# Decay column as the bias of an exponential on ScalarE instead of a sum on GpSimd, in a hybrid decoder layer

## The chip, the cores and the metric

The kernel runs on one core of a Trainium2 chip. The metric is the device time of one execution in microseconds; the median of several executions is compared. The core's engines work side by side, each through its own queue in order: TensorE (PE; its weight loads are listed as PEld), VectorE (DVE), ScalarE (ACT) and GpSimd (POOL). SyncE (SP) issues the DMA transfers.

## What is computed

The layer (sequence 512, model width 2048, one sequence) has two parallel branches: sliding-window attention with 32 query heads, and a gated delta rule ("DeltaNet") with 16 key heads and 32 value heads of 128. The change concerns the decay of the second branch:

```python
g = jnp.cumsum(g, axis=-1)
tril = jnp.tril(jnp.ones((C, C), dtype=bool))
decay = jnp.exp(jnp.where(tril, g[..., :, None] - g[..., None, :], -jnp.inf))
...
L = jnp.where(strict, jnp.einsum('bhncd,bhnsd->bhncs', k_beta, k) * decay, 0.0)
...
qk = jnp.where(tril, jnp.einsum('bhncd,bhnsd->bhncs', q, k) * decay, 0.0)
q_dec = q * jnp.exp(g)[..., None]
```

So for each value head a matrix of decays is needed twice: for L, which is inverted, and for qk. The query times the exponential of g is needed once.

## The kernel before

All matrix products are float32, split into a high and a low part: `mm3` (L236) issues three matmuls, L240 to L242, for each pair of tiles. A projection tile of 128 channels by 512 positions (`channel_tile`) is 48 such matmuls that accumulate in one PSUM tile, mm. Its weights come by DMA in tiles raw and are split by `split`: ScalarE casts a half of 128x1024 to whi (L61), VectorE subtracts to get wlo (L62).

The projections follow each other on TensorE without a break, and everything else is woven between them. Each piece of side work is a generator that yields a number; `pump` is called after every second k-step of a projection and resumes each generator that has counted down. The written program gives the priorities, and a scheduler then puts each engine's instructions into the order of its queue, by its own estimate of time. At run time each engine keeps that order and waits by semaphores.

The stages are: startup; the keys of the delta rule (`delta_keys`, with `keys` once for each of 16 groups g of one key head and two value heads e); attention; the heads of the delta rule (`delta_heads`, `queries` and `values` for each of the 16 groups); and two output stages. A solver (`solve`) works on VectorE from the end of the key stage into the first groups of heads; its steps are the lines L737 and L745 on tiles A and atmp.

A decay matrix is made in tile E, 128 partitions by 4 blocks of 128 columns. In `queries` the variable for it is M, and the profile calls it E as well:

- `decay_load` (L695) sends, for head h, the row of g to all partitions by DMA, g_rows to E.
- `decay_mask` (L701) works on GpSimd. L705 adds the column neg_g, which holds minus g for each partition and block: neg_g[:, c, h] for block c. L706 is an affine selection that puts -1e30 into the upper or lower part that is not wanted.
- The exponential is one ScalarE instruction of 128x512 for each E, at L670 in `keys` and L833 in `queries`.
- The result is multiplied on VectorE with the product of keys (L678) or of query and key (L845).

In `queries` GpSimd also multiplies the query with the exponential of g, in tile qe (L839, called qd in the code), after a DMA has brought that row (eg_rows). The value tiles go through a convolution on ScalarE and VectorE: L570, L573 three times, the tanh L578, and L580. TensorE then transposes yv (L281, tile ptv) and ScalarE copies the result (L789). L270 is the eviction of a gate projection (tanh into mth). L660 scales the keys k by a column, L668 copies their transpose kT, and L675 multiplies keys with keys (pkk).

`behind` (L244) adds a dependence for the scheduler alone: the given instruction is not placed ahead of the last matmul that has been written. It adds no wait at run time.

Of the kernel before, what the change touches and what calls it, by code (L numbers as in the profile page):

```python
# [10 lines left out]
AF = mybir.ActivationFunctionType  # L11
ALU = mybir.AluOpType
# [4 lines left out]
P = 128  # L17
# [3 lines left out]
NTB = T // P  # L21
# [24 lines left out]
class Layer:  # L46
# [194 lines left out]
        nc.tensor.matmul(ps, lhsT=wh, rhs=xl, start=False, stop=False)  # L241
        self.last_mm = nc.tensor.matmul(ps, lhsT=wl, rhs=xh, start=False, stop=last)  # L242

    def behind(self, ins):  # L244

        self.tc.add_manual_dep(
            ins.ins, self.last_mm.ins.name, mybir.DependencyInfo(mybir.DependencyClass.NoSync, mybir.DependencyReason.DATA),
            reason="pace",
        )

# [393 lines left out]
    def keys(self, wk, g, ps):  # L644

        nc = self.nc
        y = wk.tile([P, T], F32, tag="y", name="y", bufs=3)
        yield from self.conv(wk, ps, 16 + g, y)
        yield 2
        pt = self.ptp.tile([P, T], F32, tag="tp", name="ptk")  # L650
        self.transpose4(pt, lambda c: y[:, c * P : (c + 1) * P])
        ss = self.sumsq(wk, pt)
        yield 3
        E = [self.decay_load(wk, 2 * g + e) for e in range(2)]
        nc.vector.tensor_scalar(out=ss, in0=ss, scalar1=EPS, scalar2=None, op0=ALU.add)
        rk = self.rsqrt(wk, ss, NTB, "rk")
        yield 4
        k = wk.tile([P, NTB, P], F32, tag="k", name="k")
        for c in range(NTB):
            nc.scalar.activation(k[:, c, :], pt[:, c * P : (c + 1) * P], AF.Copy, scale=rk[:, c : c + 1])  # L660
        for e in range(2):
            self.decay_mask(E[e], 2 * g + e)
        yield 4
        pt = self.ptp.tile([P, T], F32, tag="tp", name="ptkT")
        self.transpose4(pt, lambda c: k[:, c, :])
        nc.sync.dma_start(out=self.k_d[g], in_=k.rearrange("p c d -> p (c d)"))
        kT = wk.tile([P, T], F32, tag="kT", name="kT")
        nc.scalar.copy(out=kT, in_=pt)  # L668
        for e in range(2):
            nc.scalar.activation(E[e], E[e], AF.Exp)  # L670
        yield 2
        pk = self.ptp.tile([P, NTB, P], F32, tag="tp", name="pkk")
        for c in range(NTB):
            sl = slice(c * P, (c + 1) * P)
            nc.tensor.matmul(pk[:, c, :], lhsT=kT[:, sl], rhs=kT[:, sl], start=True, stop=True)  # L675
        nc.sync.dma_start(out=self.kT_d[g], in_=kT)
        for e in range(2):
            nc.vector.tensor_tensor(out=E[e], in0=pk, in1=E[e], op=ALU.mult)  # L678
        yield 2
        for e in range(2):  # L680
            h = 2 * g + e
            b, hl = h // 16, h % 16
            for k2 in range(2):
                s = slice(k2 * HD, (k2 + 1) * HD)
                nc.sync.dma_start(out=self.lt_d[b, k2, hl].rearrange("c j i -> j c i"), in_=E[e][s, :, s])
            nc.sync.dma_start(out=self.lab_d[h], in_=E[e][0:HD, :, HD:P])
        self.keys_done.append(g)
# [10 lines left out]
        self.nc.sync.dma_start(out=E.rearrange("p c i -> p (c i)"), in_=self.g_rows[h].partition_broadcast(P))  # L698
        return E

    def decay_mask(self, E, h):  # L701

        nc = self.nc
        ng = self.neg_g[:, :, h].unsqueeze(2).to_broadcast([P, NTB, P])
        nc.gpsimd.tensor_tensor(out=E, in0=E, in1=ng, op=ALU.add)  # L705
        nc.gpsimd.affine_select(  # L706
            out=E, in_=E, pattern=[[0, NTB], [1, P]], compare_op=ALU.is_ge, fill=NEG, base=0, channel_multiplier=-1
        )

    def solve(self, wk, b, eng):  # L710

# [80 lines left out]
    def queries(self, wk, g, ps, st):  # L792

        nc = self.nc
        sl = lambda c: slice(c * P, (c + 1) * P)
        q = wk.tile([P, T], F32, tag="y", name="yq", bufs=3)
        yield from self.conv(wk, ps, g, q)
        M = [self.decay_load(wk, 2 * g + e) for e in range(2)]
        kT = wk.tile([P, T], F32, tag="kT", name="kT")
        nc.sync.dma_start(out=kT, in_=self.kT_d[g])  # L800
        yield 2
        pt = self.ptp.tile([P, T], F32, tag="tp", name="ptq")
        self.transpose4(pt, lambda c: q[:, sl(c)])
        ss = self.sumsq(wk, pt)
        yield 3
        epsq = wk.tile([P, NTB], F32, tag="epsq", name="epsq")
        nc.vector.tensor_scalar(out=epsq, in0=ss, scalar1=EPS, scalar2=EPS * P, op0=ALU.add, op1=ALU.mult)
        yield 1
        for e in range(2):
            self.decay_mask(M[e], 2 * g + e)  # L810
        ta = wk.tile([P, NTB, HD], F32, tag="ta", name="ta", bufs=1)
        lab = wk.tile([P, NTB, HD], F32, tag="lab", name="lab", bufs=1)
        ts1 = wk.tile([P, NTB, HD], F32, tag="ts1", name="ts1", bufs=1)
        qd, TT = [], []
        for e in range(2):
            h = 2 * g + e
            qe = wk.tile([P, NTB, P], F32, tag="qe", name="qe", bufs=2)
            nc.sync.dma_start(out=qe.rearrange("p c i -> p (c i)"), in_=self.eg_rows[h].partition_broadcast(P))
            qd.append(qe)
            b, hl = h // 16, h % 16  # L820
            t = self.tt[h % 4]
            for k2 in range(2):
                s = slice(k2 * HD, (k2 + 1) * HD)
                nc.sync.dma_start(out=t[s, :, s], in_=self.ts_d[b, k2, hl].rearrange("c j i -> j c i"))
            s = slice(e * HD, (e + 1) * HD)
            nc.sync.dma_start(out=ta[s], in_=self.ta_d[b, hl].rearrange("c i j -> i c j"))
            nc.sync.dma_start(out=lab[s], in_=self.lab_d[h])
            if e:
                nc.sync.dma_start(out=ts1[0:HD], in_=self.ts_d[b, 1, hl].rearrange("c j i -> j c i"))
            TT.append(t)  # L830
        yield 3
        for e in range(2):
            nc.scalar.activation(M[e], M[e], AF.Exp)  # L833
        k = wk.tile([P, NTB, P], F32, tag="k", name="k")
        nc.sync.dma_start(out=k.rearrange("p c d -> p (c d)"), in_=self.k_d[g])
        yield 1
        for e in range(2):
            qf = qd[e].rearrange("p c i -> p (c i)")
            nc.gpsimd.tensor_tensor(out=qf, in0=qf, in1=q, op=ALU.mult)  # L839
        yield 1  # L840
        pqk = self.ptp.tile([P, NTB, P], F32, tag="tp", name="pqk")
        for c in range(NTB):
            nc.tensor.matmul(pqk[:, c, :], lhsT=kT[:, sl(c)], rhs=q[:, sl(c)], start=True, stop=True)
        for e in range(2):
            nc.vector.tensor_tensor(out=M[e], in0=pqk, in1=M[e], op=ALU.mult)  # L845
        yield 2
        py = self.ptp.tile([P, NTB, HD], F32, tag="tp", name="py")
        own = [slice(0, HD), slice(HD, P)]
        for c in range(NTB):
            for e in range(2):  # L850
                nc.tensor.matmul(py[own[1 - e], c, :], lhsT=lab[own[e], c, :], rhs=ta[own[e], c, :], start=True, stop=True)
        Y = wk.tile([P, NTB, HD], F32, tag="Y", name="Y", bufs=1)
        nc.vector.tensor_copy(out=Y, in_=py)
        yield 2
        pu = [self.ptp.tile([P, NTB, HD], F32, tag="tp", name="pu") for _ in range(2)]
        for c in range(NTB):
            nc.tensor.matmul(pu[0][0:HD, c, :], lhsT=Y[HD:P, c, :], rhs=TT[0][HD:P, c, HD:P], start=True, stop=True)
            nc.tensor.matmul(pu[1][0:HD, c, :], lhsT=Y[0:HD, c, :], rhs=ts1[0:HD, c, :], start=True, stop=True)
        for e in range(2):
            nc.vector.tensor_tensor(  # L860
                out=TT[e][0:HD, :, HD:P],
                in0=pu[e][0:HD],
                in1=self.neg_beta[0:HD, :, 2 * g + e].unsqueeze(2).to_broadcast([HD, NTB, HD]),
                op=ALU.mult,
            )
        yield 2
        while "v1" not in st:
            yield 1
        yield 2
        yield from self.scan(wk, g, k, kT, TT, qd, M, epsq, st)  # L870
# [655 lines left out]
```

## Time and profile before

| | |
|---|---|
| median of 3 runs | 2947.74 us (2945.24 to 2948.3) |
| the profiled execution | 2939.34 us |
| its span, first to last instruction | 2937.5 us |
| mean granted TensorE clock | 0.993 |
| sums on GpSimd (L705) | 64, 78.3 us busy |
| selections on GpSimd (L706) | 64, 49.0 us busy |
| query products on GpSimd (L839) | 32, 51.1 us busy |
| exponentials of E on ScalarE (L670, L833) | 64, 40.5 us busy |

In a row of the profile, a tile's name stands ahead of the arrow with what is written and behind it with what is read; "128x512 f32" is partitions by elements. A number in brackets or behind the bar is the time for which the engine sat idle ahead of the instruction, and the arrow there names what ended that time. The granted clock is 1.00 when TensorE runs at full speed.

### The profile page before, as it was taken

How to read it: one execution, taken by the hardware profiler on the slowest of the kernel's cores; microseconds unless marked ns; L12 is line 12 of the kernel's file. 1: busy time of each engine (PE TensorE's matmuls, PEld its weight loads, DVE VectorE, ACT ScalarE, POOL GpSimd, SP SyncE). 2: the span in 40 equal slices, each digit the busy share in tenths (PEclk: the TensorE clock that was granted, in tenths of full speed). 3: DMA queues.
4: the chain of work that ended last, by engine and by line, in shares of the span. 5: the costliest groups of instructions: out<-in, count | busy, mean ns of one | idle time of the engine just before them, and what ended most of it. 6: DMA issues, size and time to landing. Idle time of an engine off the chain costs nothing.

```text
span 2937.5 us, 37979 instructions
## 1 busy us (share of the span) xinstructions
PE 2865.5 (98%) x14524; PEld 2350.7 (80%) x14524; DVE 1764.5 (60%) x2903; ACT 1088.3 (37%) x2103; POOL 208.6 (7%) x188
## 2 busy tenths in 40 slices
PE   6899999999999999999999999999999999999999
PEld 5678888887877877877888888888887887888887
DVE  5866666868768666666644444545435555434666
ACT  3355443234444333333433333333333232222443
POOL 0013210100000011111000000001000000000000
PEclk8999999999999999999999999999999999999999
DMA  9856654322252343333443333333338998855794
GB/s 334 321 166 201 197 157 145 122 78 98 85 145 96 101 144 109 123 109 109 143 136 110 122 109 123 116 123 127 106 120 296 311 327 297 297 174 176 240 323 171
DMA packets 184872, 498.32 MB, mean 170 GB/s; under 512 B 75217, under 2 KB 77777, under 8 KB 147313
## 3 DMA queue, kind: packets, MB, share of 16 engines
q1 hardware_dynamic: 184690, 495.90, 50.7%
q8 instruction: 114, 1.87, 0.3%
q14 instruction: 68, 0.56, 0.1%
HBM read 415.26 MB, written 78.33 MB: 168 GB/s over the span
## 4 chain that ended last, share of the span: by engine, by line
PE 85%; DMA 6%; DVE 4%; ACT 2%; issue 1%; POOL 1%; SPq 0%; POOLq 0%; DVEq 0%; ACTq 0%
PE mm L240 23%; PE mm L242 22%; PE mm L241 22%; DMA gw<-in_w_ada_gate 2%; PE m L242 2%; PE m L240 2%; PE m L241 2%; DMA oraw<-o_d 2%; DVE wa L410 1%; PE S L1206 1%; PE pv L892 1%; PE po L911 1%; PE O L1257 1%; PE pP L281 1%; PE po L910 1%
## 5 line engine op out<-in xcount | busy, mean ns | idle before, releaser
L240 PE MATMUL mm<-hh,whi 128*128 128x512 f32 x2784 | 1133.9, 407 | 5.2 <-ACT mth L270 5.2
L242 PE MATMUL mm<-hh,wlo 128*128 128x512 f32 x2784 | 1091.1, 392 | 0.0
L241 PE MATMUL mm<-hl,whi 128*128 128x512 f32 x2784 | 1088.7, 391 | 0.0
L62 DVE TENSOR_TENSOR wlo<-raw,whi 128x1024 fp32r<-128x1024 f32 (+1 forms) x484 | 596.4, 1233 | 490.8 <-ACT whi L61 473.4
L61 ACT CAST whi<-raw 128x1024 fp32r<-128x1024 f32 (+1 forms) x484 | 504.2, 1043 | 895.9 <-PE mm L241 778.4
L240 PEld LDWEIGHTS mm<-hh,whi 128*128 128x128 f32 x2784 | 524.8, 188 | 114.7 <-issue 8.3
L242 PEld LDWEIGHTS mm<-hh,wlo 128*128 128x128 f32 x2784 | 523.8, 188 | 114.7 <-issue 0.5
L241 PEld LDWEIGHTS mm<-hl,whi 128*128 128x128 f32 x2784 | 525.4, 189 | 98.5 <-issue 0.5
L240 PE MATMUL mm<-oh,whi 128*128 128x512 f32 x512 | 201.7, 395 | 6.2 <-ACT oh L61 6.2
L241 PE MATMUL mm<-ol,whi 128*128 128x512 f32 x512 | 200.5, 392 | 0.4 <-DVE ol L62 0.4
L242 PE MATMUL mm<-oh,wlo 128*128 128x512 f32 x512 | 200.2, 391 | 0.0
L240 PEld LDWEIGHTS mm<-oh,whi 128*128 128x128 f32 x512 | 96.6, 189 | 28.4 <-ACT oh L61 7.5
L839 POOL TENSOR_TENSOR qe<-qe,yq 128x512 f32<-128x512 f32 x32 | 51.1, 1616 | 931.4 <-DMA qe<-eg_rows 743.5
L241 PEld LDWEIGHTS mm<-ol,whi 128*128 128x128 f32 x512 | 96.8, 189 | 22.2 <-DVE ol L62 1.3
L242 PEld LDWEIGHTS mm<-oh,wlo 128*128 128x128 f32 x512 | 96.7, 189 | 20.2
L745 DVE TENSOR_TENSOR A<-A,atmp 128x62 f32<-128x62 f32 (+30 forms) x124 | 111.1, 896 | 0.6
L737 DVE TENSOR_TENSOR atmp<-A 128x62 f32<-128x62 f32 (+30 forms) x124 | 109.3, 882 | 0.6
L705 POOL TENSOR_TENSOR E<-E,neg_g 128x512 f32<-128x512 f32 x64 | 78.3, 1223 | 391.8 <-DMA E<-g_rows 352.1
L885 DVE SCALAR_TENSOR_TENSOR r<-pp,neg_eg,vt 128x128 f32<-128x128 f32 x96 | 29.2, 346 | 86.3 <-PE pp L882 84.8
L1230 ACT ACTIVATE sm<-sm,mx,rs 128x256 f32<-128x256 f32 (+1 forms) x128 | 71.7, 562 | 3.8 <-DVE mx L1225 3.8
L573 DVE SCALAR_TENSOR_TENSOR yv<-mm,convh,yv 128x511 f32<-128x511 f32 (+2 forms) x96 | 71.3, 742 | 1.4
L1433 DVE SCALAR_TENSOR_TENSOR gate_bc<-gw,silu_c,gate_bc 128x2048 f32<-128x2048 f32 x15 | 35.2, 2350 | 42.1 <-DMA gw<-in_w_ada_gate 42.1
(337 smaller groups left out, 3015.5 us busy)
## 6 DMA issues: line engine op xcount, KB each, us to landing
raw<-in_w_ch SPq DMA_DIRECT2D x158, 1024.0 KB
wa<-in_w_ada_ss SPq DMA_DIRECT2D x32, 1024.0 KB
raw<-in_w_od SPq DMA_DIRECT2D x32, 1024.0 KB
E<-g_rows SPq DMA_DIRECT2D x64, 256.0 KB
q<-in_w_out SPq DMA_DIRECT2D x32, 512.0 KB
gw<-in_w_ada_gate SPq DMA_DIRECT2D x16, 1024.0 KB
f_d<-q SPq DMA_DIRECT2D x32, 512.0 KB
raw<-in_w_os SPq DMA_DIRECT2D x16, 1024.0 KB
```

Source lines behind the costliest of these rows:

```text
L61: self.nc.scalar.copy(out=hi, in_=src)
L62: self.nc.vector.tensor_tensor(out=lo, in0=src, in1=hi.bitcast(F32), op=ALU.subtract)
L240: nc.tensor.matmul(ps, lhsT=wh, rhs=xh, start=first, stop=False)
L241: nc.tensor.matmul(ps, lhsT=wh, rhs=xl, start=False, stop=False)
L242: self.last_mm = nc.tensor.matmul(ps, lhsT=wl, rhs=xh, start=False, stop=last)
L573: nc.vector.scalar_tensor_tensor(out=y[:, s:], in0=ps[:, : T - s], scalar=w[:, j : j + 1], in1=y[:, s:], op0=ALU.mult, op1=ALU.add)
L705: nc.gpsimd.tensor_tensor(out=E, in0=E, in1=ng, op=ALU.add)
L737: eng.tensor_tensor(out=t, in0=A[:, m : m + 1, m + 1 :].to_broadcast([P, m, n]), in1=A[:, :m, m : m + 1].to_broadcast([P, m, n]), op=ALU.mult,
L745: self.behind(eng.tensor_tensor(out=A[:, :m, m + 1 :], in0=A[:, :m, m + 1 :], in1=t, op=ALU.add))
L839: nc.gpsimd.tensor_tensor(out=qf, in0=qf, in1=q, op=ALU.mult)
L1230: nc.scalar.activation(t, t, AF.Exp, scale=r[:, h : h + 1], bias=mx[:, h : h + 1], accum_out=den[:, h : h + 1])
L1433: nc.vector.scalar_tensor_tensor(out=acc, in0=w, scalar=s, in1=acc, op0=ALU.mult, op1=ALU.add)
```

## The change

The sum on GpSimd goes. The selection works on the row of g alone, and the exponential adds the column as its bias. A bias is one column of 128 partitions, and each of the four blocks has its own, so one exponential of 128x512 becomes four of 128x128. Since the masked places hold -1e30, the bias added there afterwards changes nothing in the result. In `queries` the products qe now carry a scheduler dependence on the last selection of the same group.

```diff
-    def behind(self, ins):
+    def behind(self, ins, other=None):
         self.tc.add_manual_dep(
-            ins.ins, self.last_mm.ins.name, ...
+            ins.ins, (other or self.last_mm).ins.name, ...
...
         for e in range(2):
-            self.decay_mask(E[e], 2 * g + e)
+            self.decay_mask(E[e])
...
         for e in range(2):
-            nc.scalar.activation(E[e], E[e], AF.Exp)
+            self.decay_exp(E[e], 2 * g + e)
...
-    def decay_mask(self, E, h):
-        nc = self.nc
-        ng = self.neg_g[:, :, h].unsqueeze(2).to_broadcast([P, NTB, P])
-        nc.gpsimd.tensor_tensor(out=E, in0=E, in1=ng, op=ALU.add)
-        nc.gpsimd.affine_select(
+    def decay_mask(self, E):
+        self.last_mask = self.nc.gpsimd.affine_select(
             out=E, in_=E, pattern=[[0, NTB], [1, P]], compare_op=ALU.is_ge, fill=NEG, base=0, channel_multiplier=-1
         )
+    def decay_exp(self, E, h):
+        for c in range(NTB):
+            self.nc.scalar.activation(E[:, c, :], E[:, c, :], AF.Exp, bias=self.neg_g[:, c, h : h + 1])
...
         for e in range(2):
-            self.decay_mask(M[e], 2 * g + e)
+            self.decay_mask(M[e])
+        masks = self.last_mask
...
         for e in range(2):
-            nc.scalar.activation(M[e], M[e], AF.Exp)
+            self.decay_exp(M[e], 2 * g + e)
...
-            nc.gpsimd.tensor_tensor(out=qf, in0=qf, in1=q, op=ALU.mult)
+            self.behind(nc.gpsimd.tensor_tensor(out=qf, in0=qf, in1=q, op=ALU.mult), masks)
```

The order of instructions in the queues, at three places. A row gives line, operation, and what is written and read; the lines of the changed kernel are two off those of the one before, from the middle of `queries` on.

GpSimd's queue in the heads stage, at the second and third groups, before the change; the numbers behind the names tell the buffers apart, and yq is the query:

```order
L839 TENSOR_TENSOR qe_9817<-qe_9817,yq_9651 128x512
L839 TENSOR_TENSOR qe_9823<-qe_9823,yq_9651 128x512
L705 TENSOR_TENSOR E_10272<-E_10272,neg_g_1262 128x512
L706 AFFINE_SELECT E_10272<-E_10272 128x512
L705 TENSOR_TENSOR E_10274<-E_10274,neg_g_1262 128x512
L706 AFFINE_SELECT E_10274<-E_10274 128x512
L839 TENSOR_TENSOR qe_10388<-qe_10388,yq_10221 128x512
L839 TENSOR_TENSOR qe_10394<-qe_10394,yq_10221 128x512
```

The same place with the change:

```order
L841 TENSOR_TENSOR qe_9883<-qe_9883,yq_9719 128x512
L841 TENSOR_TENSOR qe_9889<-qe_9889,yq_9719 128x512
L703 AFFINE_SELECT E_10344<-E_10344 128x512
L703 AFFINE_SELECT E_10346<-E_10346 128x512
L841 TENSOR_TENSOR qe_10458<-qe_10458,yq_10293 128x512
L841 TENSOR_TENSOR qe_10464<-qe_10464,yq_10293 128x512
```

The two sums are gone. The query products already stood behind their own group's selections and still do; the selections of a group stand behind the products of the group ahead of it.

ScalarE's queue in the heads stage, where the exponentials of the third group stand between two steps of a value tile (yv), before the change:

```order
L693 ACTIVATE junk,ss<-ptq 128x128 x4
L61 CAST whi<-raw 128x1024
L570 ACTIVATE yv<-mm,convh 128x512
L833 ACTIVATE E<-E 128x512 x2
L61 CAST whi<-raw 128x1024
L578 ACTIVATE th<-yv 128x512
L789 COPY vt<-ptv 128x512
```

And with the change:

```order
L693 ACTIVATE junk,ss<-ptq 128x128 x4
L61 CAST whi<-raw 128x1024
L570 ACTIVATE yv<-mm,convh 128x512
L709 ACTIVATE E<-E,neg_g 128x128 x8
L61 CAST whi<-raw 128x1024
L578 ACTIVATE th<-yv 128x512
L790 COPY vt<-ptv 128x512
```

Two exponentials have become eight at the same place, ahead of the cast and the tanh.

ScalarE's queue at the beginning of the heads stage, before the change; mth is the eviction of a gate projection:

```order
L61 CAST whi<-raw 128x1024
L833 ACTIVATE E<-E 128x512 x2
L61 CAST whi<-raw 128x1024
L270 ACTIVATE mth<-mm 128x512
L61 CAST whi<-raw 128x1024 x2
L570 ACTIVATE yq<-mm,convh 128x512
L833 ACTIVATE E<-E 128x512
L61 CAST whi<-raw 128x1024
L578 ACTIVATE th<-yq 128x512
```

And with the change:

```order
L61 CAST whi<-raw 128x1024
L709 ACTIVATE E<-E,neg_g 128x128 x7
L61 CAST whi<-raw 128x1024
L270 ACTIVATE mth<-mm 128x512
L709 ACTIVATE E<-E,neg_g 128x128
L61 CAST whi<-raw 128x1024 x2
L570 ACTIVATE yq<-mm,convh 128x512
L709 ACTIVATE E<-E,neg_g 128x128 x5
L578 ACTIVATE th<-yq 128x512
```

Seven of the first group's eight exponentials stand ahead of the cast and the eviction, one behind them; the tanh of the query now stands ahead of a cast that it stood behind. TensorE's order is the same in both kernels, and SyncE's differs in one place of the key stage, where two transfers are swapped.

More of the change, by code (lines that the diff above doesn't have):

```diff
@@ L242, in mm3 @@
         self.last_mm = nc.tensor.matmul(ps, lhsT=wl, rhs=xh, start=False, stop=last)
-    def behind(self, ins):
+    def behind(self, ins, other=None):
         self.tc.add_manual_dep(
-            ins.ins, self.last_mm.ins.name, mybir.DependencyInfo(mybir.DependencyClass.NoSync, mybir.DependencyReason.DATA),
+            ins.ins, (other or self.last_mm).ins.name, mybir.DependencyInfo(mybir.DependencyClass.NoSync, mybir.DependencyReason.DATA),
             reason="pace",
```

## Prediction, made before the changed kernel ran

> **What bounds the kernel now.** I read the totals first, then the busy time by stage, then who is waited for on TensorE.
>
> ```profile
> span 2937.5 us, 37979 instructions
> PE 2865.5 (98%) x14524; PEld 2350.7 (80%) x14524; DVE 1764.5 (60%) x2903; ACT 1088.3 (37%) x2103; POOL 208.6 (7%) x188
> ```
>
> TensorE (PE) is busy for 2865.5 of 2937.5 us, so all its idle time is 72 us. GpSimd (POOL) is busy 7%: making it faster is worth nothing by itself. Only idle time of TensorE, or time in which its clock is cut, can be won. The windows below give, after each stretch and its length, busy us with the count for PE, PEld, DVE, ACT and POOL, then granted clock, DMA share and GB/s. The key stage lies in the first (with attention), the first five groups of heads in the second, the other groups in the third.
>
> ```profile
> 160.00:1050.00 890.00, 888.86 (x4659) 722.63 (x4658) 629.59 (x1142) 380.68 (x814) 98.60 (x84) 1.00 0.42 131
> 1050.00:1400.00 350.00, 334.99 (x1739) 276.41 (x1738) 222.29 (x349) 119.53 (x256) 44.03 (x38) 0.98 0.38 122
> 1400.00:2190.00 790.00, 790.00 (x4161) 658.01 (x4160) 393.65 (x746) 299.27 (x656) 65.74 (x62) 1.00 0.37 119
> ```
>
> Where decay masks are made, TensorE is idle 1.1 us in the first stretch, 15.0 us in the second (350 less 334.99, at a clock of 0.98) and not at all in the third. The other 56 us lie in stages without decay masks. So 16 us of idle time, and what the clock loses in the second stretch, are the most that can be won. The waits of TensorE, first in 160 to 560 us, then in 1040 to 2200 us:
>
> ```profile
> PE pkk L675 <- ACT kT L668: 0.8, 1, 0.8
> ```
>
> ```profile
> PE ptv L281 <- DVE yv L580: 10.9, 4, 2.9
> PE mm L240 <- ACT mth L270: 5.2, 2, 3.8
> ```
>
> Four waits before the transpose of a value tile and a long one for an eviction. Here is the first of the four in the timeline, by TensorE, GpSimd, ScalarE (ACT) and VectorE (DVE): start, length, engine, line, and in brackets the idle time before it.
>
> ```profile
> 1173.29 0.63 PE L281 MATMUL ptv<-ident,yv 128*128 128x128 f32 x4 [2.69 <-DVE yv L580]
> ```
>
> ```profile
> 1162.37 3.49 POOL L839 TENSOR_TENSOR qe<-qe,yq 128x512 f32<-128x512 f32 x2 [67.28 <-DMA qe<-eg_rows]
> 1165.83 2.02 POOL L705 TENSOR_TENSOR E<-E,neg_g 128x512 f32<-128x512 f32 x1
> 1167.93 0.64 POOL L706 TENSOR_SCALAR_AFFINE_SELECT E<-E 128x512 f32<-128x512 f32 x1
> 1168.53 1.05 POOL L705 TENSOR_TENSOR E<-E,neg_g 128x512 f32<-128x512 f32 x1
> 1169.65 0.63 POOL L706 TENSOR_SCALAR_AFFINE_SELECT E<-E 128x512 f32<-128x512 f32 x1
> ```
>
> ```profile
> 1168.59 0.63 ACT L833 ACTIVATE E<-E 128x512 f32<-128x512 f32 x1 [6.66 <-POOL E L706]
> 1170.32 0.63 ACT L833 ACTIVATE E<-E 128x512 f32<-128x512 f32 x1 [1.09 <-POOL E L706]
> 1170.86 1.03 ACT L61 CAST whi<-raw 128x1024 fp32r<-128x1024 f32 x1
> 1171.79 0.62 ACT L578 ACTIVATE th<-yv 128x512 f32<-128x512 f32 x1
> ```
>
> ```profile
> 1165.29 1.66 DVE L62 TENSOR_TENSOR wlo<-raw,whi 128x1024 fp32r<-128x1024 f32 x1
> 1172.45 0.69 DVE L580 SCALAR_TENSOR_TENSOR yv<-th,yv 128x512 f32<-128x512 f32 x1 [3.65 <-ACT th L578]
> ```
>
> Read backwards: TensorE waits for yv, yv for the tanh (L578), and that tanh stands in ScalarE's queue behind two exponentials, which wait for GpSimd. GpSimd ends its query products at 1165.83 and then runs sum, selection, sum, selection. So here the two sums are on the path, though GpSimd idles nearly always. The other stalls with the same mark:
>
> ```profile
> 1069.19 0.69 PE L240 MATMUL mm<-hh,whi 128*128 128x512 f32 x1 [3.84 <-ACT mth L270]
> ```
>
> ```profile
> 1243.33 1.02 PE L281 MATMUL ptv<-ident,yv 128*128 128x128 f32 x4 [2.58 <-DVE yv L580]
> ```
>
> ```profile
> 1315.28 1.09 PE L281 MATMUL ptv<-ident,yv 128*128 128x128 f32 x4 [2.89 <-DVE yv L580]
> ```
>
> ```profile
> 1387.04 1.09 PE L281 MATMUL ptv<-ident,yv 128*128 128x128 f32 x4 [2.76 <-DVE yv L580]
> ```
>
> **Price of the new instructions.** The groups by line with shapes kept apart, and the instructions that touch tile E (shortest, median, longest ns):
>
> ```profile
> L833 ACT ACTIVATE E<-E 128x512 f32<-128x512 f32 x32 | 20.3, 633 | 95.4 <-POOL E L706 95.3
> L660 ACT ACTIVATE k<-ptk,rky 128x128 f32<-128x128 f32 x64 | 18.6, 370 | 26.9 <-DVE rky L73 26.9
> L774 ACT ACTIVATE zh<-mm,dnwh 128x512 f32<-128x512 f32 x32 | 22.0, 689 | 0.0
> L427 ACT ACTIVATE h<-xnT,sh 128x512 f32<-128x512 f32 x16 | 13.1, 816 | 62.8 <-DVE sh L422 62.8
> ```
>
> ```profile
> L705 POOL TENSOR_TENSOR E<-E,neg_g x64: 1039/1051/2025, 177.5 to 2058.0; 128x512 f32<-128x512 f32 x64
> L706 POOL TENSOR_SCALAR_AFFINE_SELECT E<-E x64: 634/635/1577, 178.6 to 2059.1; 128x512 f32<-128x512 f32 x64
> ```
>
> An exponential over 128 columns with a column as bias is not in the trace. Lower end: L660, 128 columns with a column as scale, 0.370. Upper end: L774 less L660 is 0.319 for 384 columns, so an exponential of 128 columns without a column would be 0.633 - 0.319 = 0.314; L427, with a column for scale and one for bias, is 0.183 over L833, so half of that for one: 0.405. Neighbours on ScalarE overlap by 0.09 (the exponential of 0.63 at 1170.32 is followed at 1170.86), so one costs 0.28 to 0.32 of the queue. I take 0.29, nearer to L660, which is the same size and has one column. Two tiles then take 8 x 0.29 = 2.32 where they took 2 x 0.54 = 1.08: ScalarE gains 1.24 us of work a pair, 40 us over 32 pairs. VectorE and DMA get no new instruction, and the order of TensorE is unchanged.
>
> **The four stalls.** The sum of 2.02 is 0.97 longer than its median of 1.05: it starts while VectorE runs the two-input L62, and ends about 1.05 after that has ended. I take it that a selection put in its place is held just as long, since selections too run up to 1.577. From the end of the hold (1166.80) to the cast (1170.86) the path was 4.06. Now it is one selection, 0.64, a gap of some 0.03, and eight exponentials, 2.32, together 2.99; the second selection runs under the first four exponentials (0.64 under 1.16). Gain 1.07 a stall; 0.83 to 1.15 with 0.32 and 0.28 for an exponential. If the selection is not held, 0.97 more at this stall.
>
> The Trainium skill has a rule on this: its page "SBUF — State Buffer", section "Who interferes with whom", says that VectorE and GpSimd share a port pair as an exclusive lock, and that a two-input VectorE instruction contends with any GpSimd instruction that reads SBUF. By that rule the selection is held like the sum and the gain is 1.07; without it 2.04. The trace agrees with the rule as far as the 2.02 beside the 1.66 shows it.
>
> Four stalls: 4 x 1.07 = 4.3. What is late next is the same chain, yv behind the tanh: stalls of about 1.6, 1.5, 1.8 and 1.7 remain.
>
> **The long stall.** At 1069.19 the eviction L270 stands behind two exponentials and a cast. Its two sums:
>
> ```profile
> 1061.77 1.18 POOL L705 TENSOR_TENSOR E<-E,neg_g 128x512 f32<-128x512 f32 x1 [6.32 <-DMA E<-g_rows]
> 1063.02 1.42 POOL L706 TENSOR_SCALAR_AFFINE_SELECT E<-E 128x512 f32<-128x512 f32 x1
> 1064.40 1.93 POOL L705 TENSOR_TENSOR E<-E,neg_g 128x512 f32<-128x512 f32 x1
> ```
>
> They leave, 3.11; seven exponentials now stand ahead of the cast in place of two, 2.03 for 1.08. Gain 2.2 (1.1, as at the others, if the sum's hold goes over to the selection). About 1.6 of 3.84 remains. The wait of 0.8 in the key stage, also behind exponentials that follow four sums, should go: 0.8.
>
> **The clock.** After four of the five stalls the first transposes take 1.02 to 1.09 (or the first matmul 0.69), where after the 2.69 stall they take 0.63: the clock is halved for a while. The same 18 matmuls stand between each transpose and these rows:
>
> ```profile
> 1175.94 0.48 PE L240 MATMUL mm<-hh,whi 128*128 128x512 f32 x1
> ```
>
> ```profile
> 1247.57 0.47 PE L240 MATMUL mm<-hh,whi 128*128 128x512 f32 x1
> ```
>
> 2.65 from 1173.29, 4.24 from 1243.33: 1.6 lost, 6.4 for four. Does it come back? Two shorter stalls elsewhere:
>
> ```profile
> 2198.71 0.50 PE L240 MATMUL mm<-hh,whi 128*128 128x512 f32 x1 [1.41 <-ACT mth L270]
> ```
>
> ```profile
> 2435.86 0.51 PE L240 MATMUL mm<-oh,whi 128*128 128x512 f32 x1 [1.80 <-ACT oh L61]
> ```
>
> After 1.41 and 1.80 the matmul runs at the full clock (0.50). The stalls that remain are at most 1.8, so I take all 6.4.
>
> **The second edit**, query products behind the selections, I cost at nothing: in GpSimd's queue they stood there already, only the sums are gone between. No queue is passed and no wait added.
>
> **Sum.** 4.3 + 2.2 + 0.8 + 6.4 = 13.7, say 14. The profiled execution took 2939.34 (span 2937.5 and 1.8 around it), so 2925.3; the median shown, 2947.74, is 8.4 above it, and I carry the 14 over to it: **2933.7**. Such a kernel can be told from no change by about 0.2%, 5.9 us.
>
> **Rivals.**
> - The clock stays halved: the shortened stalls still trip it. For it: 2.58 trips and 2.69 does not, so length alone does not decide. Against it: 1.41 and 1.80 above. Gain then 7.3: 2940.4. The Trainium skill, "TensorE: Matmul & The Clock Gate", Part 1, gives a free-running window of about 3.4 us and a cut after an idle one; here stalls of 2.58 to 2.89 were cut already, so the rows differ from that length.
> - The selections are not held: 4 x 1.0 more at most: 17.6, 2930.
> - The change does not do what it says: the eight exponentials take the place of the sums. An exponential would have to cost (4.06 - 0.67) / 8 = 0.42 of the queue, above my upper end of 0.32. Stalls and clock stay: within 2 us, 2947.
> - Slower: where ScalarE finds its masks ready, it gains nothing and pays 1.24 a pair, and the key stage follows ScalarE (kT and k lie behind it). It speaks for this that not all exponentials wait:
>
> ```profile
> ACT E L833 <- POOL E L706: 95.3, 31, 6.7
> ACT E L670 <- POOL E L706: 49.0, 25, 4.8
> ```
>
>   31 of 32 in the heads wait for GpSimd, 25 of 32 in the key stage. If TensorE had no slack there, 16 pairs would cost 20 us against 14: 2953.6. It decides from the point where 1.24 exceeds ScalarE's lead over TensorE in the key stage; against it, TensorE waits there once, for 0.8, and ScalarE is busy 43% (380.68 of 890).
>
> **How the numbers follow.** Forecast (gain 10 to 17) 0.58, clock stays 0.15, not held 0.10, no effect 0.10, slower 0.07. Faster by over 0.2%: the forecast, the unheld case and most of the clock case, 0.80; within 0.2% 0.13; slower 0.07. Range: down by the unheld case and some of the 3 us between the shown runs (2945.24 to 2948.3), 2925; up by the clock case and the lower gains (0.83 a stall, 1.1 for the long one: 2 us less), 2943. The no-effect and slower cases are left out.
>
> **What would show it.** Right: GpSimd's E lines fall from 64 sums and 64 selections to 64 selections; the stalls at the value transposes shrink from 2.6-2.9 to about 1.6, their transposes take 0.63, and the clock in the second stretch is 1.00. Wrong: transposes of 1.0 (clock stays), selections of 0.64 there with stalls of 0.7 (not held), exponentials of over 0.5, or waits of TensorE for kT or k in the key stage.

## The result, and the profile after

| | before | after |
|---|---|---|
| median | 2947.67 us (2945.24 to 2949.59, 6 runs) | 2929.55 us (2926.36 to 2930.57, 6 runs) |
| the profiled execution | 2939.34 us | 2929.78 us |
| its span | 2937.5 us | 2928.0 us |

The ratio of the two kernels' runs is 0.9937, with a 95% interval from 0.9925 to 0.995: the change makes the kernel faster by 18.1 us (15 to 22). The forecast was 2933.7, a gain of 14. The two profiled executions differ by 9.6 us only; what is known of the rest comes with the experiments.

The totals and the same three stretches of the changed kernel (the second begins where the heads begin), in the columns of before:

```profile
span 2928.0 us, 38184 instructions
...
PE 2861.4 (98%) x14524; PEld 2346.6 (80%) x14524; DVE 1755.9 (60%) x2903; ACT 1128.6 (39%) x2295; POOL 130.9 (4%) x124
```

```profile
160.00:1050.00 890.00, 889.61 (x4663) 723.76 (x4662) 623.79 (x1146) 401.25 (x911) 53.81 (x52) 1.00 0.42 131
1050.00:1400.00 350.00, 341.11 (x1792) 282.07 (x1791) 229.94 (x365) 132.03 (x298) 31.16 (x26) 1.00 0.39 125
1400.00:2190.00 790.00, 788.59 (x4152) 656.47 (x4151) 387.91 (x734) 309.48 (x714) 45.68 (x42) 1.00 0.38 121
```

ScalarE has 40 us more work (1128.6 for 1088.3, as worked out) and GpSimd 78 less, and neither number is the gain. The gain is in TensorE's idle time of the second stretch: 8.9 us (350 less 341.11) where it was 15.0, and in its clock there, 1.00 where it was 0.98. The 1.4 us that the third stretch is idle is no loss: it is the wait of 1.41 that stood at 2198.71 before, and now comes ahead of 2190. The waits of TensorE between 1030 and 2190 us (total, times, longest) say the same:

```profile
PE ptv L281 <- DVE yv L580: 7.5, 4, 2.5
PE mm L240 <- ACT mth L270: 2.8, 2, 1.4
```

They were 10.9 and 5.2 (up to 2200 us, so that both counts hold that wait of 1.41), and the wait of 0.8 in the key stage is gone: 6.6 us of idle time. The five stalls one by one, in TensorE's timeline (idle time in the brackets):

```profile
1067.45 0.50 PE L240 MATMUL mm<-hh,whi 128*128 128x512 f32 x1 [1.41 <-ACT mth L270]
```

```profile
1168.51 0.63 PE L281 MATMUL ptv<-ident,yv 128*128 128x128 f32 x4 [1.67 <-DVE yv L580]
```

```profile
1237.57 0.63 PE L281 MATMUL ptv<-ident,yv 128*128 128x128 f32 x4 [1.57 <-DVE yv L580]
```

```profile
1307.56 1.09 PE L281 MATMUL ptv<-ident,yv 128*128 128x128 f32 x4 [2.49 <-DVE yv L580]
```

```profile
1378.13 0.63 PE L281 MATMUL ptv<-ident,yv 128*128 128x128 f32 x4 [1.76 <-DVE yv L580]
```

The first of these rows is the long stall, the others are the four before the value transposes. The long one fell from 3.84 to 1.41, three of the four from 2.6-2.8 to 1.6-1.8, the third only to 2.49, and behind that one alone the transposes still run slow (1.09).

The chain ahead of the first of the four, in the timelines of GpSimd, VectorE and ScalarE:

```profile
1162.06 2.21 POOL L703 TENSOR_SCALAR_AFFINE_SELECT E<-E 128x512 f32<-128x512 f32 x2
```

```profile
1161.53 1.66 DVE L62 TENSOR_TENSOR wlo<-raw,whi 128x1024 fp32r<-128x1024 f32 x1
```

```profile
1163.72 2.46 ACT L709 ACTIVATE E<-E,neg_g 128x128 f32<-128x128 f32 x8 [5.54 <-POOL E L703]
1166.08 1.04 ACT L61 CAST whi<-raw 128x1024 fp32r<-128x1024 f32 x1
1167.02 0.62 ACT L578 ACTIVATE th<-yv 128x512 f32<-128x512 f32 x1
```

The two selections take 2.21 where two of 0.64 would be some 1.2 (neighbours overlap a little), beside the same L62: the selection is held about 1.0, as the sum was (0.97). The eight exponentials take 2.46. In the rows of tile E, one takes (shortest, median, longest ns):

```profile
L709 ACT ACTIVATE E<-E,neg_g x256: 385/389/430, 180.0 to 2050.0; 128x128 f32<-128x128 f32 x128
```

So the next one follows (2.46 - 0.389) / 7 = 0.296 later: 0.29 had been taken. The tanh still stands where it stood, behind all of them.

### The profile page after: what moved, and what is told of

Its sections match the earlier page's. It is cut to its first block, busy times and chain, and to the rows that moved or that the text cites. A ratio compares the mean times of both kernels' runs of the same rounds, so it can differ in the third digit from the quotient of the medians.

```text
span 2928.0 us, 38184 instructions
## 1 busy us (share of the span) xinstructions
PE 2861.4 (98%) x14524; PEld 2346.6 (80%) x14524; DVE 1755.9 (60%) x2903; ACT 1128.6 (39%) x2295; POOL 130.9 (4%) x124
## 4 chain that ended last, share of the span: by engine, by line
PE 86%; DMA 5%; DVE 5%; ACT 2%; issue 1%; SPq 0%; POOL 0%; DVEq 0%; POOLq 0%; ACTq 0%
PE mm L240 23%; PE mm L242 23%; PE mm L241 23%; DMA oraw<-o_d 2%; PE m L241 2%; PE m L242 2%; PE m L240 2%; DMA gw<-in_w_ada_gate 1%; DVE wa L410 1%; PE pv L894 1%; PE po L913 1%; PE O L1259 1%; PE S L1208 1%; PE pP L281 1%; ACT sm L1232 1%
## 5 line engine op out<-in xcount | busy, mean ns | idle before, releaser
L62 DVE TENSOR_TENSOR wlo<-raw,whi 128x1024 fp32r<-128x1024 f32 (+1 forms) x484 | 597.5, 1235 | 485.8 <-ACT whi L61 470.0
L709 ACT ACTIVATE E<-E,neg_g 128x128 f32<-128x128 f32 x256 | 82.3, 394 | 86.0 <-POOL E L703 86.0
L703 POOL TENSOR_SCALAR_AFFINE_SELECT E<-E 128x512 f32<-128x512 f32 x64 | 48.2, 767 | 436.4 <-DMA E<-g_rows 366.1
```

Source lines behind the costliest of these rows:

```text
L62: self.nc.vector.tensor_tensor(out=lo, in0=src, in1=hi.bitcast(F32), op=ALU.subtract)
L703: self.last_mask = self.nc.gpsimd.affine_select(out=E, in_=E, pattern=[[0, NTB], [1, P]], compare_op=ALU.is_ge, fill=NEG, base=0, channel_ ...
L709: self.nc.scalar.activation(E[:, c, :], E[:, c, :], AF.Exp, bias=self.neg_g[:, c, h : h + 1])
```

## The experiments

Two questions were open. Is it this chain, GpSimd to exponentials to tanh to transpose, that costs the time, or something else that the change brings along (less GpSimd work beside VectorE, another form of exponential, the key stage)? And what decides when the clock is cut? Medians of one group below come from one chip, each with the kernel before on that chip (its median in the table); the ratio is to that.

| kernel | median, us | before, us | ratio, 95% interval |
|---|---|---|---|
| before_look (one run) | 2943.52 | 2944.26 | |
| split_only | 2944.94 | 2944.26 | 1.0006 (0.9997 to 1.0016) |
| select_twice | 2938.95 | 2944.26 | 0.998 (0.9969 to 0.9992) |
| after_again | 2932.11 | 2946.82 | 0.9951 (0.9937 to 0.9965) |
| tanh_first | 2923.43 | 2946.82 | 0.9919 (0.9904 to 0.9933) |
| before_tanh_first | 2924.04 | 2946.82 | 0.9921 (0.9907 to 0.9935) |
| keys_only | 2943.38 | 2944.06 | 1.0 (0.9991 to 1.0008) |
| heads_only | 2930.76 | 2944.06 | 0.9957 (0.9943 to 0.997) |

**The tanh ahead of the exponentials.** The changed kernel with a dependence for the scheduler, so that the heads' exponentials stand behind the tanh in ScalarE's queue (the weight cast that stood between them comes ahead of them too):

```diff
-        nc.scalar.activation(th, y, AF.Tanh)
+        self.last_th = nc.scalar.activation(th, y, AF.Tanh)
...
         for c in range(NTB):
-            self.nc.scalar.activation(E[:, c, :], E[:, c, :], AF.Exp, bias=self.neg_g[:, c, h : h + 1])
+            x = self.nc.scalar.activation(E[:, c, :], E[:, c, :], AF.Exp, bias=self.neg_g[:, c, h : h + 1])
+            if other is not None:
+                self.behind(x, other)
...
-            self.decay_exp(M[e], 2 * g + e)
+            self.decay_exp(M[e], 2 * g + e, self.last_th)
```

> The changed kernel with a dependence for the scheduler that puts the heads' exponentials behind the tanh of the value tile, so that ScalarE's queue at the stalls has casts and tanh ahead of the eight exponentials. Theory (the tanh waits only because it stands behind exponentials that wait for GpSimd): the four remaining stalls (7.5 us idle in the trace of the changed kernel, less what the chain needs anyway) and the cut clock after the third of them (1.6) go: 8 to 10 us, 2919 to 2922. What could be late next is the product of query and key that needs the decays, or the copy of the value tile behind the exponentials (2.3 us of ScalarE). Rival (the stalls are of another origin, or the exponentials' delay returns at the copy behind them): no gain, or stalls under another name; 2929.

Measured: 2923.43 (2920.22 to 2924.75), 8.7 below the changed kernel on the same chip (2932.11). Its waits of TensorE between 1030 and 2190 us, whole, and its second stretch:

```profile
PE mm L240 <- ACT mth L270: 2.8, 2, 1.4
```

```profile
1050.00:1400.00 350.00, 348.59 (x1837) 289.18 (x1836) 231.16 (x372) 137.40 (x302) 30.95 (x26) 1.00 0.40 129
```

All four stalls before the value transposes are gone, and no other takes their place; 1.4 us of idle time is left in the stretch that had 15.0. It is the long stall, still 1.41, though no exponential stands ahead of the gate eviction any more. The cast just ahead of that eviction waits for TensorE itself:

```profile
1065.04 1.04 ACT L61 CAST whi<-raw 128x1024 fp32r<-128x1024 f32 x1 [4.38 <-PE mm L241]
```

So the 1.41 that the change left there stands without exponentials too. Why the other four are gone, ScalarE's timeline shows at the place of the first: the tanh no longer waits for GpSimd.

```profile
1161.29 1.05 ACT L61 CAST whi<-raw 128x1024 fp32r<-128x1024 f32 x1 [3.92 <-PE mm L241]
1163.14 0.64 ACT L578 ACTIVATE th<-yv 128x512 f32<-128x512 f32 x1 [0.81 <-DVE yv L573]
1163.68 2.44 ACT L709 ACTIVATE E<-E,neg_g 128x128 f32<-128x128 f32 x8
```

**The same without the change.** The kernel before, sums and single exponentials kept, only that order (the tanh is kept in last_th as above):

```diff
...
-            nc.scalar.activation(M[e], M[e], AF.Exp)
+            self.behind(nc.scalar.activation(M[e], M[e], AF.Exp), self.last_th)
```

> The kernel before, sums and single exponentials kept, with the same dependence: exponentials of the heads behind the tanh. Theory (the sums cost time only through the tanh that waits behind them): the sums are then hidden, the 10.9 us of stalls and the clock that is cut after them (4.8 to 6.4) go, and the time comes within some 2 us of the changed kernel with the same dependence, 2920 to 2926 (the stall behind the gate eviction, 5.2, and its clock may stay: then 2926). Rival (taking the sums off GpSimd is worth time by itself, through memory or port): it stays 6 or more above the changed kernel with this order.

Measured: 2924.04 (2922.49 to 2929.29), 0.6 above tanh_first, far within the runs' spread. So with the tanh ahead, taking the sums off GpSimd is worth some 2 us or less (0.6 between the medians, 1.9 between the means, 1.6 in the waits of the trace); the change gains because it shortens what an ill-placed tanh waits for. The long stall is 1.41 here too, since this order moves the first group's exponentials behind the gate eviction. The waits that stay:

```profile
PE mm L240 <- ACT mth L270: 2.8, 2, 1.4
PE ptv L281 <- DVE yv L580: 1.6, 2, 0.9
```

The last row is two waits, of 0.86 and 0.74, at the third and fourth of the places where before stalled. Here is the first of them, with the rows of VectorE and GpSimd ahead of it:

```profile
1302.95 0.63 PE L281 MATMUL ptv<-ident,yv 128*128 128x128 f32 x4 [0.86 <-DVE yv L580]
```

```profile
1299.82 1.95 DVE L62 TENSOR_TENSOR wlo<-raw,whi 128x1024 fp32r<-128x1024 f32 x1
1301.69 1.12 DVE L580 SCALAR_TENSOR_TENSOR yv<-th,yv 128x512 f32<-128x512 f32 x1
```

```profile
1299.64 1.05 POOL L705 TENSOR_TENSOR E<-E,neg_g 128x512 f32<-128x512 f32 x1
1300.76 1.50 POOL L706 TENSOR_SCALAR_AFFINE_SELECT E<-E 128x512 f32<-128x512 f32 x1
```

The second sum and the selection behind it now run beside L62 and L580, which are longer by 0.74 and 0.44 than at the same place of tanh_first, where GpSimd is done by then and TensorE does not wait:

```profile
1298.37 1.21 DVE L62 TENSOR_TENSOR wlo<-raw,whi 128x1024 fp32r<-128x1024 f32 x1
1299.50 0.68 DVE L580 SCALAR_TENSOR_TENSOR yv<-th,yv 128x512 f32<-128x512 f32 x1
```

**The base of these two, once more.**

> The changed kernel once more on the chip of the two kernels with the tanh first, as their base: 2929.6, with four stalls before the value transposes of 1.6, 1.6, 2.5 and 1.8 and one of 1.4 behind the gate eviction, if its first profile was a typical one. If the stall of 2.5 is chance, it is nearer to 1.8 here and its transposes take 0.63.

Measured: 2932.11 (2928.85 to 2937.25), 14.7 below before on that chip. Its waits before the value transposes are 6.9 in all, the longest 1.9, and all four transposes take 0.63: the 2.49 of the first profile was a chance of that execution. What made it is not known.

**One part each.** The change in the key stage alone (for tile E) and in the heads alone (for tile M); decay_select is the selection without the sum:

```diff
-            self.decay_mask(E[e], 2 * g + e)
+            self.decay_select(E[e])
...
-            nc.scalar.activation(E[e], E[e], AF.Exp)
+            self.decay_exp(E[e], 2 * g + e)
```

> The kernel before with the change in the key stage alone: there the sums are gone and four exponentials with a column as bias stand in place of one; the heads keep sums and single exponentials. Theory (in the key stage neither GpSimd nor ScalarE is on the path but for one wait of 0.8): at most 0.8 faster, so the time of before within 1 us; the five stalls of the heads as before (2.6 to 2.9, and 3.8). Rival (the key stage follows ScalarE, which gets 1.24 more for each of 16 pairs): up to 20 us slower, with waits of TensorE for kT or k. Second rival (the 32 sums gone from the key stage free a port or memory for VectorE): over 2 us faster. On the clock: in all eight traces so far the spells of half clock begin on a grid of 3.41 us, and a slot of that grid in the heads in which TensorE is busy for 1.5 us or less is followed by one, a slot with 1.7 or more by none; a trace of this kernel should sort its stalls the same way, whatever their length.

> The kernel before with the change in the heads alone; the key stage keeps sums and single exponentials. Theory (all but 0.8 of the gain is won at the five stalls of the heads): the time of the changed kernel within 1 to 2 us, 15 us below before, with stalls of 1.6 to 2.5 before the value transposes and 1.4 behind the gate eviction. Rival (part of the gain beyond 10 to 13 us, by which the profiled executions differ, comes from the key stage): 5 us or more above the changed kernel. On the clock the same as for the key stage alone: spells of half clock behind grid slots with 1.5 us or less of TensorE work, none behind slots with 1.7 or more.

Measured: the key stage alone gives nothing (ratio 1.0, 0.9991 to 1.0008), the heads alone 13.3 us (0.9957), as much as the whole change within the intervals. In the key stage the change brings ScalarE 20 us of work and TensorE no wait: the first stretch of keys_only, where before had 380.68 for ScalarE:

```profile
160.00:1050.00 890.00, 889.60 (x4664) 724.15 (x4663) 623.77 (x1142) 400.48 (x911) 53.44 (x52) 1.00 0.42 131
```

And heads_only still has the one wait of the key stage:

```profile
PE pkk L675 <- ACT kT L668: 0.8, 1, 0.8
```

**Four exponentials without a bias.**

```diff
-            nc.scalar.activation(M[e], M[e], AF.Exp)
+            for c in range(NTB):
+                nc.scalar.activation(M[e][:, c, :], M[e][:, c, :], AF.Exp)
```

The same in the key stage; the sums stay.

> The kernel before, sums on GpSimd kept, with each exponential cut into four of 128x128 without a bias. Theory (the chain GpSimd, exponentials, tanh, VectorE, transpose sets the stalls): the four exponentials of the second tile cost about 4 x 0.29 = 1.16 where one of 0.63 stood, so each of the four stalls grows by about 0.6 and the long one too: 3.2 us, and 1.6 more if the first stall (2.69) now trips the clock as well; some 3 to 5 us slower than before, 2951 to 2952 where before has 2947.7. Rival (the gain of the change comes from GpSimd's smaller use of memory and port, or from the form of the exponential, and not from this chain): the stalls stay and the time is that of before. Second rival (ScalarE's load bounds the other stages): over 10 us slower.

Measured: 2944.94, from 0.9 faster to 4.7 slower by the interval: the time alone doesn't tell the theories apart. The trace does. Two rows of ScalarE ahead of the first stall, and the stall:

```profile
1170.15 0.91 ACT L835 ACTIVATE E<-E 128x128 f32<-128x128 f32 x4 [6.78 <-POOL E L707]
1171.88 0.91 ACT L835 ACTIVATE E<-E 128x128 f32<-128x128 f32 x4 [0.82 <-POOL E L707]
```

```profile
1175.12 1.09 PE L281 MATMUL ptv<-ident,yv 128*128 128x128 f32 x4 [3.08 <-DVE yv L580]
```

Four of them take 0.91, not the 1.16 of the expectation: 0.28 more than the one of 0.63, and the four stalls grew by 0.28 to 0.39 each (12.2 us in all for 10.9). The long stall, which should have grown too, did so by 0.07 only (3.91 for 3.84). So at the four stalls the chain passes a delay on about one to one, and the expectation had the price too high: 0.29 is that of an exponential with a bias. Without one the next follows after (0.91 - 0.295) / 3 = 0.205, by its row of tile E:

```profile
L835 ACT ACTIVATE E<-E x128: 292/295/313, 1065.9 to 2067.0; 128x128 f32<-128x128 f32 x128
```

**Each selection twice.**

```diff
-        self.last_mask = self.nc.gpsimd.affine_select(
+        for _ in range(2):
+            self.last_mask = self.nc.gpsimd.affine_select(
```

> The changed kernel with each selection issued twice on GpSimd; the second finds everything done and changes nothing. Theory (GpSimd's work before the exponentials lies on the path of the stalls): the second selection of a tile adds about 0.64 ahead of its exponentials; the first tile's is on the path, the second tile's two run under the first tile's exponentials (1.28 against 1.16), so each stall grows by 0.65 to 0.8, from 1.57-1.76 to about 2.3, and from 2.49 to about 3.2: 3 to 4 us, and up to 1.6 for each stall that trips the clock again; 2933 to 2938. Rival (GpSimd's work is hidden once the sums are gone, and the remaining stalls come from ScalarE alone): 2929.6, stalls unchanged.

Measured: 2938.95 (2927.03 to 2944.86), 5.3 below before on its chip, where the changed kernel was 14.7 and 18.1 below on others: some 9 us or more given back, at or above the upper end. Its waits of TensorE:

```profile
PE ptv L281 <- DVE yv L580: 9.3, 4, 2.5
PE mm L240 <- ACT mth L270: 2.8, 1, 2.8
```

The four stalls are 2.2 to 2.6 long and the long one 2.77, twice its 1.41. GpSimd's work is on the path still. The idle time grew by 3 to 4 us (9.3 for 6.9 to 7.5, and 1.4 at the long stall); the clock has most of the rest, as follows.

**Before, a second profile, and the clock.**

> The kernel before once more, unchanged, to see a second profile of it. The profiled execution of before took 2939.34 us, 8 less than the median of its runs, while that of the changed kernel (2929.78) sits on its median. If the profiled execution was an odd one, this profile takes about 2947 and shows about 8 us more of idle time or cut clock in places that the first did not have, and these places are then part of what the change wins. If it was not odd, and profiles of before run shorter than its timed runs, this one takes about 2939 again, with the same five stalls of TensorE (10.9 us before the value transposes, 5.2 before the matmuls behind the gate eviction).

Measured: 2943.52, between the two, with the same five stalls (11.0 us before the value transposes). Its stretches of half clock are 51.0 us long in all, those of the first profile 38.7. Both have four in the heads; the others lie in the start and in the output stages, which the change does not touch. Each run comes with its mean granted clock, so its time splits into what a cut clock lost (time x (1 - clock)) and the rest. Means over the runs, in us (a run's clock is given in thousandths, which is 3 us, so only means are of use; a difference between two rows is good to some 2 to 3 us):

| | runs | lost to the clock | rest |
|---|---|---|---|
| before, on three chips | 23, 9, 15 | 22.7, 23.6, 23.0 | 2921.4, 2923.3, 2921.2 |
| split_only | 11 | 23.6 | 2922.3 |
| keys_only | 11 | 22.5 | 2921.6 |
| select_twice | 12 | 21.3 | 2916.6 |
| after, after_again | 6, 5 | 14.6, 17.0 | 2914.5, 2915.5 |
| heads_only | 5 | 15.8 | 2915.7 |
| before_tanh_first | 5 | 15.2 | 2909.6 |
| tanh_first | 4 | 15.3 | 2907.6 |

On the chip of after_again the change won 23.6 - 17.0 = 6.6 us of clock and 2923.3 - 2915.5 = 7.8 of the rest, 14.4 between the means (14.7 between the medians). The first profiled execution of before lost half of its 38.7 us at half clock, 19.3, and has a rest of 2920.0: 3 to 4 us below the means of its kernel in the clock and 1 to 3 in the rest. So the two profiled executions show less of the gain than the medians. Whether a usual run of before has 1 to 3 us more idle time, and where, was not found.

What cuts the clock can be seen in stretches of 3.41 us. First before, at the stalls of 2.69 and 2.58; the second column is the length, the third TensorE's busy time, the 1.00 or 0.50 behind the fifth engine the granted clock:

```profile
1168.32:1171.73 3.41, 2.28 (x11) 1.54 (x9) 0.48 (x1) 2.04 (x3) 1.89 (x3) 1.00 0.42 156
1171.73:1175.15 3.42, 1.86 (x11) 1.65 (x12) 2.70 (x3) 1.32 (x4) 0.00 (x0) 1.00 0.00 0
1240.00:1243.41 3.41, 0.83 (x5) 0.40 (x4) 0.92 (x2) 2.10 (x3) 0.33 (x1) 1.00 0.14 53
1243.41:1246.83 3.42, 3.42 (x11) 2.84 (x12) 1.93 (x2) 0.90 (x2) 0.00 (x0) 0.50 0.39 96
```

The longer stall, at 1173.29, lies across two stretches and leaves TensorE 2.28 and 1.86 of work in them; the shorter lies in one whole and leaves 0.83, and the next stretch, exactly, has half the clock. In keys_only the first stall, of 2.69 again, lies otherwise, and now it is followed by a cut:

```profile
1168.64:1172.06 3.42, 1.12 (x5) 0.58 (x4) 0.46 (x1) 2.10 (x3) 0.73 (x2) 1.00 0.29 108
1172.06:1175.47 3.41, 3.03 (x10) 2.57 (x11) 2.47 (x3) 0.59 (x1) 0.00 (x0) 0.50 0.34 53
```

So it goes in all ten traces: within a trace the cuts begin a multiple of 3.41 us apart. In the heads, a stretch at full clock with 1.46 us of work or less was always followed by one, with 1.54 or more never. The nearest on each side, in select_twice and in after:

```profile
1165.03:1168.45 3.42, 1.54 (x7) 0.94 (x5) 0.51 (x1) 3.17 (x8) 0.39 (x1) 1.00 0.41 153
1168.45:1171.86 3.41, 3.08 (x20) 2.82 (x21) 2.60 (x4) 1.85 (x3) 0.00 (x0) 1.00 0.32 46
```

```profile
1303.60:1307.02 3.42, 1.46 (x7) 0.88 (x5) 1.44 (x2) 2.48 (x6) 0.00 (x0) 1.00 0.41 153
1307.02:1310.43 3.41, 2.88 (x9) 2.52 (x10) 2.21 (x3) 0.59 (x1) 0.00 (x0) 0.50 0.71 240
```

The bounds of keys_only's and heads_only's expectation (1.5 and 1.7) held in the heads of both. In the output stages behind 2190 us they are less sharp: there a stretch with 1.88 was followed by a cut and one with 1.60 by none. A cut stretch costs half its length, 1.7 us, and one that has idle time of its own can be followed by another: the 3.08 of split_only cost two. How the stretches lie differs from run to run, so a stall of less than 3.41 - 1.5 = 1.9 us, with TensorE busy on both sides of it, costs its length alone, and a longer one 1.7 more in some of the runs. This fits select_twice: its stalls of 2.2 to 2.8 lie above 1.9, those of the changed kernel below, mostly; its runs spread over 18 us and lost 21.3 us to the clock.

## Why the prediction was right

- **The path.** Right, and shown: with the tanh ahead, the four stalls vanish in both kernels, by an edit that leaves TensorE's and GpSimd's order alone and puts the exponentials of the heads behind the tanh.
- **The exponential's price.** 0.29 taken, 0.296 measured; its ends (0.28, 0.32) hold it. The upper bound without a column, 0.314, was 0.295.
- **The hold of the selection by L62.** Taken as 0.97, seen as about 1.0 at the first stall. That was read in the traces; a kernel without L62 there was not tried. The sum of before ends 0.90 behind L62 (1167.85 against 1166.95), not 1.05 as the prediction reads; the end of the hold, 1166.80, is counted back from the sum's own end and does not depend on it. The Trainium skill's rule ("SBUF — State Buffer", "Who interferes with whom"), that a VectorE instruction with two inputs in SBUF contends with a GpSimd instruction that reads SBUF, agrees with it, and before_tanh_first shows it from the other side: there VectorE's two-input L62 and L580 were longer beside the sum and the selection (1.95 for 1.21, 1.12 for 0.68).
- **The four stalls.** 4.3 forecast; 10.9 - 7.5 = 3.4 in the first profile and 10.9 - 6.9 = 4.0 in the second. The remainders 1.6, 1.5, 1.8, 1.7 came out as 1.67, 1.57, 2.49 (1.89 in the second) and 1.76.
- **The long stall.** 2.2 forecast, 3.84 - 1.41 = 2.4. That it fits is in part luck: the 1.6 that was to remain stood for exponentials, and the 1.41 that does remain is there without any ahead of the eviction (tanh_first).
- **The key stage.** 0.8 forecast and found (in the trace); too small for the time to show.
- **The clock.** 6.4 forecast, from four cuts of 1.6. In the first pair of profiles four cuts became one, 5.1; over the runs 6.6. The size was right, the reason half, so that the size is in part luck: "the stalls that remain are at most 1.8" is right since 1.9 is the bound, but 1.41 and 1.80 elsewhere could not give that bound, and the prediction had no account of why 2.58 was cut and 2.69 not.
- **The second edit.** Nothing, as forecast: heads_only has no such dependence, and its GpSimd queue has the same order in the heads as that of the changed kernel.
- **The sum.** 13.7 forecast as 7.3 of idle time and 6.4 of clock; 14.7 measured on one chip, as 7.8 and 6.6 between the means, and 18.1 on the first. The forecast lies below the first interval (15 to 22) by about 1 us and within the second (10 to 19). Its weak step was the last: it carried a gain from one execution to the median, and that execution was a quick one, 3 to 4 us below its kernel's means in the clock and 1 to 3 in the rest.

Of the rivals, the clock that stays cut came true at one stall of one profile; the selection that is not held (stalls of 0.7 were to remain, 1.57 and more do), the change without effect and the slower key stage are refuted by the rows above and by keys_only.

## What to carry to other kernels

Ask of a stall not only which engine ends last but whether the waiting instruction had to stand behind that engine's consumer: here an order with the tanh first, in a few lines, hid nearly all of the sums and gave 23 us, where speeding up what stood ahead of the tanh gave 13 to 18, and some 2 or less on top of that order. Keep the stalls of TensorE below the length that can cut the clock (here 1.9 us): one just above it costs up to 1.7 more. A profiled execution is one draw; carry its terms to a median only with the granted clock of several runs beside it.

## What the runs showed of the hardware

The clock is cut in fixed stretches of 3.41 us, by the work in the stretch before and not by the length of a stall: from full clock, half the clock follows a stretch with 1.46 us of TensorE work or less, and does not follow one with 1.54 or more (in the heads; in the output stages the two overlap: 1.88 was followed, 1.60 was not). The length is that which the Trainium skill gives ("TensorE: Matmul & The Clock Gate", Part 1: a free-running window of 3413 ns); that a window must be idle, as it says, is not what the traces show, where one 43% busy (1.46 of 3.41) was enough. And a column as the bias of an exponential of 128 columns has a price: 389 ns for 295, and 0.296 for 0.205 in a row of them; of what ScalarE pays for a tile here, 4 x 0.091 = 0.36 is the column and 0.91 - 0.63 = 0.28 the cut into four.
